# Product tiles of an S5 stage moved from SBUF to PSUM, beside the scan's multipliers

## The chip, the cores and the metric

The kernel runs on one core of a Trainium2 chip. The metric is device time of one execution, in microseconds (us). Engines: PE (TensorE), DVE (VectorE), ACT (ScalarE), POOL (GpSimd); SP is SyncE, whose queue issues all DMAs here. SBUF is the working memory; PSUM is where PE writes, eight banks of 512 float32 columns per partition.

## The reference

Two layers over a latent stream and a context stream of 256 tokens each, 1024 features. Layer 0 mixes tokens by a bidirectional diagonal complex state space (S5): 64 groups of 16 channels with 64 complex states each.

```
a_bar = exp(lam * dt)
b_bar = ((a_bar - 1) / lam)[..., None] * B
h[l]  = a_bar * h[l - 1] + b_bar @ u[l]        # both directions
y     = real(C @ h) + D * u;  out = glu(gelu(y) @ w_glu)
```

The context is scanned first; the latents' scan starts from the context's last state. Then comes a squared-ReLU MLP. Layer 1 is a gated delta rule with an MLP of its own. Every sub-layer has an RMS norm, a modulation by rows computed from c (the `ada` products), and a gated residual.

## The kernel before

The stage of interest is the S5 mixer of layer 0, some 300 us out of the whole. Tokens are cut into 64 chunks of 8 positions, 32 of the context and 32 of the latents, and the work goes by 8 batches of 8 groups.

- `s5_powers` (line 549) computes the powers a^1 .. a^8 (`pw`) and the inputs' factors (`eb`) on DVE. Its last lines allocate the tile `scan`, one PSUM bank, and write a^8 into its first 256 columns by eight small copies (real part and signed imaginary part, per half of the pairs); the tile `scanm`, 256 columns in SBUF, is for the scan's products.
- `s5_we` (line 706) spreads a batch's factors over the partitions by matmuls, into PSUM (`ebx`).
- `s5_w` (line 713) makes, per batch and direction, the tile `W` of 8 positions x 8 groups x 16 channels by `mul_bc` (line 686). That runs twice over half of the positions, 512 columns each time: wtmp = ebx[re] x bc, W = ebx[im] x bc, W = W + wtmp. `wtmp` is one SBUF tile. There are 32 such triples, all on DVE. A small ACT copy takes one position of each W for later (`W0`).
- `s5_in` (line 730) transposes W on PE (`sint`), copies it out by ACT (`Sin`), multiplies it by the tokens U (`xin`), and ACT copies the chunk inputs into X.
- `s5_v` (line 773) makes the outputs' powers V by the same three operations, 1024 columns each, on POOL, with all operands in SBUF (`vtmp`, `bcC`, `ec`). The next batch's `bcC` is loaded into a ring of two tiles.
- `s5_k` (line 790) multiplies V and W0 into strips, stores a strip to DRAM (`kd`), and loads it back eight times, shifted (`Kt`). There is one strip tile; four rounds, for two batches each. Products of Kt and U (`yl`) are the chunks' own part of the outputs.
- `s5_scan` (line 891) goes over the chunks, 63 steps, all on DVE. A step is eight operations of 64 columns: four products m = X[n] x a^8 (`scanm<-X,scan`), then four sums X[n + 1] += m (`X<-X,scanm`), two per half of the pairs.
- `s5_out` (line 909) multiplies the states by V (`yp`), per batch and stream; the context's outputs need the first 31 steps, the latents' all 63. A DVE transpose (`yT`) and a split in two (`y_split`, `yl<-yT,yh`) follow, then the GLU, whose weights are split into a high half on ACT (`whi`) and a low half (`wlo`) on POOL and DVE.

Every operation is recorded by one helper, so all stand under line 254; the rows are read by tile names. The order of the work on each engine is fixed when the program is built: `drive` emits the steps of the tasks in the order in which they could start by a rough clock, each with a priority (the scan 0, outputs 1, `s5_w` 3, `s5_in` 4, `s5_v` 5, strips 7), and a planner then orders each engine's queue by its own model of time. At run time every queue is strictly in order. In `s5_phase` (line 1241) a first part runs to the end of the chunk inputs; a second part has the scan, the rest of V and of the strips, and the context's outputs.

## Time and profile before

| what | us |
|---|---|
| median of 3 runs | 1667.96 |
| lowest, highest | 1667.34, 1669.84 |
| span of the profiled execution, first to last instruction | 1666.9 |

| engine | busy us | share of the span |
|---|---|---|
| PE | 1475.8 | 89% |
| DVE | 1148.8 | 69% |
| ACT | 761.4 | 46% |
| POOL | 663.2 | 40% |

The times are those of whole executions; the span is what one profiled execution took between its first and last instruction, and every duration below comes from that one. Busy shares are means over stages that differ; a stretch of the timeline says more. A wait that the profile shows on an engine holds up all that stands behind it in that engine's queue.

### The profile page before, as it was taken

The numbers are of one execution on the slowest core, as the hardware profiler recorded it, in microseconds if no ns is written. First come the engines' busy times: TensorE is split into PE (matmuls) and PEld (weight loads), VectorE is DVE, ScalarE is ACT, GpSimd is POOL, SyncE is SP. The second block draws the span as 40 slices with busy tenths as digits, with TensorE's granted clock in tenths as the row PEclk, the third lists the DMA queues.
The fourth block names the chain that finished last, engine by engine and source line by source line (L and its number), as shares of the span: only waits on it lengthen the run. The fifth ranks groups of instructions, "written<-read, shape, count | busy, mean of one in ns | idle before, by whom it ended". The sixth has DMA issues, their size and how long they took to land.

```text
span 1666.9 us, 31459 instructions
## 1 busy us (share of the span) xinstructions
PE 1475.8 (89%) x12370; PEld 1122.1 (67%) x12370; DVE 1148.8 (69%) x2267; ACT 761.4 (46%) x1637; POOL 663.2 (40%) x510
## 2 busy tenths in 40 slices
PE   6794386998999999997978898989898999989998
PEld 2464255776777777786766676767676665679997
DVE  7997879774333334337999868587769775667666
ACT  3242162644223222224455755665556764554443
POOL 3988012452333333333675734442425310014342
PEclk8797688898999999998988999999999999999999
DMA  9684743354454545521322211111111111545552
GB/s 287 216 278 90 99 135 114 116 195 140 139 183 163 176 155 172 172 105 65 97 70 73 68 56 55 52 46 39 58 52 52 50 56 48 171 147 184 181 199 89
DMA packets 76789, 201.77 MB, mean 121 GB/s; under 512 B 8544, under 2 KB 28768, under 8 KB 76384
## 3 DMA queue, kind: packets, MB, share of 16 engines
q1 hardware_dynamic: 76640, 199.75, 38.0%
q8 instruction: 97, 1.59, 0.4%
q14 instruction: 52, 0.43, 0.1%
HBM read 192.71 MB, written 7.01 MB: 120 GB/s over the span
## 4 chain that ended last, share of the span: by engine, by line
PE 61%; DVE 20%; issue 5%; ACT 5%; DMA 4%; POOL 3%; SPq 1%; POOLq 0%; DVEq 0%; ACTq 0%
PE w L254 31%; PE proj L254 8%; PE c L254 6%; DVE cacc L254 4%; PE wo L254 3%; PE ada L254 2%; PE glu L254 2%; DVE X L254 2%; DVE vc L254 1%; DVE U L254 1%; SPq L254 1%; DMA kd<-strip 1%; DVE W L254 1%; DVE gt L254 1%; PE op L254 1%
## 5 line engine op out<-in xcount | busy, mean ns | idle before, releaser
L254 ACT CAST whi<-wraw 128x1024 fp32r<-128x1024 f32 x221 | 225.6, 1045 | 262.3 <-PE w L254 139.8
L254 POOL TENSOR_TENSOR wlo<-wraw,whi 128x512 fp32r<-128x512 f32 x129 | 182.5, 1433 | 281.5 <-ACT whi L254 242.7
L254 DVE TENSOR_TENSOR wlo<-wraw,whi 128x1024 fp32r<-128x1024 f32 (+1 forms) x189 | 221.2, 1197 | 77.8 <-ACT whi L254 77.4
L254 PE MATMUL w<-hh,whi 128*128 128x256 f32 (+1 forms) x512 | 170.5, 336 | 0.0
L254 PE MATMUL w<-hl,whi 128*128 128x256 f32 (+1 forms) x512 | 169.0, 332 | 0.0
L254 PE MATMUL w<-hh,wlo 128*128 128x256 f32 (+1 forms) x512 | 168.5, 331 | 0.0
L254 POOL TENSOR_TENSOR sq<-rl 128x512 f32<-128x512 f32 (+1 forms) x64 | 62.2, 973 | 217.8 <-ACT rl L254 214.0
L254 PE MATMUL w<-whi,h1h 128*128 128x512 f32 x384 | 148.9, 395 | 0.0
L254 PE MATMUL w<-whi,h1l 128*128 128x512 f32 x384 | 148.5, 390 | 0.0
L254 PE MATMUL w<-wlo,h1h 128*128 128x512 f32 x384 | 148.4, 389 | 0.0
L254 PE MATMUL proj<-hh,whi 128*128 128x256 f32 (+1 forms) x360 | 133.0, 369 | 11.3 <-ACT pp L254 8.6
L254 DVE TENSOR_TENSOR ma<-w,g 128x512 f32<-128x512 f32 x96 | 65.3, 687 | 102.3 <-PE w L254 102.2
L254 PE MATMUL proj<-hh,wlo 128*128 128x256 f32 (+1 forms) x360 | 128.0, 356 | 1.1 <-POOL wlo L254 1.1
L254 PE MATMUL proj<-hl,whi 128*128 128x256 f32 (+1 forms) x360 | 128.9, 358 | 0.0
L254 DVE SCALAR_TENSOR_TENSOR cacc<-pp,cw,cacc 128x520 f32<-128x520 f32 (+1 forms) x128 | 114.3, 895 | 11.4 <-ACT cacc L254 9.9
L254 POOL TENSOR_TENSOR xr<-xr,ma 128x512 f32<-128x512 f32 x56 | 80.4, 1439 | 96.8 <-DVE ma L254 96.8
L254 PEld LDWEIGHTS w<-hh,whi 128*128 128x128 f32 x512 | 98.0, 192 | 18.5 <-DVE wlo L254 4.2
L254 DVE TENSOR_TENSOR h1l<-sq,h1h 128x512 fp32r<-128x512 f32 (+1 forms) x64 | 35.5, 555 | 107.4 <-POOL sq L254 104.9
L254 ACT ACTIVATE v<-c,vsc 64x128 f32<-64x128 f32 x224 | 80.6, 362 | 54.0 <-PE c L254 46.5
L254 PEld LDWEIGHTS w<-hl,whi 128*128 128x128 f32 x512 | 98.1, 192 | 10.6 <-issue 1.9
L254 PEld LDWEIGHTS w<-hh,wlo 128*128 128x128 f32 x512 | 97.8, 191 | 9.8 <-issue 0.8
L254 POOL TENSOR_TENSOR rstd<-ms,mhalf 128x1 f32<-128x1 f32 (+2 forms) x22 | 17.3, 787 | 190.2 <-DVE ms L254 190.2
(312 smaller groups left out, 3584.6 us busy)
## 6 DMA issues: line engine op xcount, KB each, us to landing
wraw<-in_w_dram SPq DMA_DIRECT2D x128, 512.0 KB, 4.2
adaw<-in_ada_w_dram SPq DMA_DIRECT2D x92, 512.0 KB, 4.4
wraw<-in_w_in_dram SPq DMA_DIRECT2D x48, 512.0 KB, 3.3
wraw<-in_w_glu_dram SPq DMA_DIRECT2D x32, 512.0 KB, 3.5
wraw<-in_w_out_dram SPq DMA_DIRECT2D x16, 512.0 KB, 3.3
Kt<-kd SPq DMA_DIRECT2D x32, 128.0 KB, 6.5
X<-grd SPq DMA_DIRECT2D x32, 128.0 KB, 3.2
V<-in_ada_w_dram SPq DMA_DIRECT2D x4, 512.0 KB, 6.7
```

The costliest lines, as they stand in the source:

```text
L254: r = f(*args, **kw)
```

## The change

The tile `wtmp` of `s5_w` becomes a PSUM tile that shares the ring of one with `scan`. The scan's products `sm` go into columns 256 to 511 of the `scan` bank, whose columns 0 to 255 hold a^8. Since the bank serves `wtmp` first, the eight copies of a^8 move out of `s5_powers` into a task of their own, `s5_a8`, behind the last `s5_w`. The SBUF tiles `wtmp` (512 columns) and `scanm` (256 columns) are gone. Nothing is computed in another way. The diff, cut to these lines (elsewhere it drops comments alone):

```diff
         cmul(eb[:, 1:8], pw[:, 0:7], eb[:, 0], 7)
-        sc = self.ps.tile([128, 512], F32, name="scan", tag="scan", bufs=1)
+    def s5_a8(self):
+
+        V, pw = self.nc.vector, self.pw
+        sc = self.bank("scan", "scan", bufs=1)
         self.a8 = sc[:, 0:256].rearrange("p (k h r d g) -> p k h r d g", k=2, h=2, r=2, d=2)
-        self.sm = self.long.tile([128, 256], F32, name="scanm").rearrange("p (h k e) -> p h k e", h=2, k=2)
+        self.sm = sc[:, 256:512].rearrange("p (h k e) -> p h k e", h=2, k=2)
         for hf in range(2):
...
             V.tensor_copy(self.a8[:, 1, hf, 1], half(1))
+        yield
...
         for d in range(2):
             yield from self.Wslots.take()
-            tmp = E.tile([128, 8, 4, 16], F32, name="wtmp", bufs=1)
+            tmp = self.bank("wtmp", "scan", bufs=1).rearrange("p (g t c) -> p g t c", g=8, t=4)
             W = self.W[b, d] = E.tile([128, 8, 8, 16], F32, name="W", bufs=NW)
...
             ins.append(T(k.s5_in(b), 4, [ws[b], u] + ins[-2:-1], "tensor"))
+        a8 = T(k.s5_a8(), 3, [ws[-1]], "vector")
...
-        rest = drive(k.clock, [lds, a0, a1, xn, u] + we + ws + ins + Ec + list(V.values()) + list(Kk.values()), until=ins + Ec)
+        rest = drive(k.clock, [lds, a0, a1, xn, u, a8] + we + ws + ins + Ec + list(V.values()) + list(Kk.values()), until=ins + Ec + [a8])
```

## Rows read from the trace of the kernel before

**Rows 1.** The page's first line.
```profile
span 1666.9 us, 31459 instructions
```
**Rows 2.** Stretches: us; busy PE, PEld, DVE, ACT, POOL (x instructions); PE clock; DMA share; GB/s.
```profile
75.00:121.00 46.00, 45.80 (x527) 29.92 (x527) 44.62 (x53) 21.35 (x60) 39.83 (x18) 0.91 0.70 237
...
141.00:218.00 77.00, 26.65 (x634) 21.47 (x630) 62.74 (x284) 12.33 (x27) 18.65 (x9) 0.65 0.61 85
218.00:281.00 63.00, 48.04 (x355) 33.75 (x348) 62.23 (x251) 28.25 (x56) 15.43 (x12) 0.84 0.40 134
281.00:375.00 94.00, 87.18 (x599) 68.19 (x598) 73.89 (x112) 51.98 (x88) 48.60 (x40) 0.95 0.47 154
```
**Rows 3.** Chain of waits, 0 to 420 us: start, length, what.
```profile
135.78 3.80 DMA bcC<-in_bc_dram
141.18 9.90 DMA kd<-strip
...
210.93 3.64 PE yl L254 x64
```
**Rows 4.** Timeline of DVE: start, us, operation, count [idle before <- releaser].
```profile
140.45 0.80 DVE L254 TENSOR_TENSOR scanm<-X,scan 128x64 f32<-128x64 f32 x4 [9.05 <-ACT X L254]
141.18 5.67 DVE L254 TENSOR_TENSOR X<-X,scanm 128x64 f32<-128x64 f32 x4
...
160.98 0.76 DVE L254 TENSOR_TENSOR X<-X,scanm 128x64 f32<-128x64 f32 x4
...
218.34 0.45 DVE L254 STREAM_TRANSPOSE yT<-yg 128x256 f32<-128x256 f32 x1 [14.59 <-ACT yg L254]
```
**Rows 5.** Stretches, instructions that touch scanm alone: us, DVE busy (x), clock, DMA.
```profile
210.00:282.00 72.00, 45.56 (x218) 0.81 0.36 119
```
**Rows 6.** Groups of DVE, 26 to 132 us: count | busy us, mean ns | idle before.
```profile
L254 DVE TENSOR_TENSOR W<-W,wtmp 128x512 f32<-128x512 f32 x32 | 44.0, 1375 | 1.0
L254 DVE TENSOR_TENSOR wtmp<-ebx,bcB 128x512 f32<-128x512 f32 x32 | 22.1, 690 | 1.3
```
**Rows 7.** Timeline of DVE, three places in the W stage.
```profile
62.55 8.56 DVE L254 TENSOR_TENSOR U<-U,md 128x1024 f32<-128x1024 f32 x4
71.03 2.82 DVE L254 TENSOR_TENSOR W<-W,wtmp 128x512 f32<-128x512 f32 x1
...
95.15 0.69 DVE L254 TENSOR_TENSOR W<-W,wtmp 128x512 f32<-128x512 f32 x1
```
**Rows 8.** Groups of POOL, 27 to 136 us, then 142 to 160.5 us.
```profile
L254 POOL TENSOR_TENSOR V<-V,vtmp 128x1024 f32<-128x1024 f32 x12 | 32.3, 2689 | 0.7
L254 POOL TENSOR_TENSOR V<-ec,bcC 128x1024 f32<-128x1024 f32 x14 | 31.7, 2285 | 6.0 <-DMA bcC<-in_bc_dram 5.6 <-issue 0.4
...
L254 POOL TENSOR_TENSOR V<-V,vtmp 128x1024 f32<-128x1024 f32 x4 | 9.4, 2340 | 0.2
...
L254 POOL TENSOR_TENSOR V<-ec,bcC 128x1024 f32<-128x1024 f32 x2 | 4.0, 2034 | 0.0
```
**Rows 9.** Timeline of DVE, copies of a^8 into the scan bank.
```profile
21.14 0.65 DVE L254 COPY scan<-pw 128x32 f32<-128x32 f32 x3
...
22.06 0.20 DVE L254 COPY scan<-pw 128x32 f32<-128x32 f32 x1
```
**Rows 10.** Timeline of ACT, 60 to 90 us.
```profile
59.82 0.39 ACT L254 COPY md<-mod 128x256 f32<-128x256 f32 x1 [1.17 <-PE mod L254]
...
73.89 0.30 ACT L254 COPY W<-W 128x128 f32<-128x128 f32 x1 [9.74 <-DVE W L254]
```
**Rows 11.** Timeline of PE, two waits.
```profile
74.78 1.12 PE L254 MATMUL sint<-consts,W 128*128 128x128 f32 x4 [3.69 <-ACT X L254]
...
258.94 0.79 PE L254 MATMUL glu<-wlo,yh 128*128 128x512 f32 x1 [8.23 <-DVE wlo L254]
```
**Rows 12.** The scan's sums on DVE, 161 to 203 us, then 218 to 281.4 us.
```profile
L254 DVE TENSOR_TENSOR X<-X,scanm 128x64 f32<-128x64 f32 x124 | 23.7, 250 | 0.0
...
L254 DVE TENSOR_TENSOR X<-X,scanm 128x64 f32<-128x64 f32 x110 | 28.5, 314 | 0.0
```

## The prediction

> **What bounds the kernel now.** I read the share of busy time by stretch first [rows 1, 2]. After 281 us TensorE (PE) is busy 87.2 of 94 us and stays so; what happens before that is the state space stage, and a microsecond won or lost there is handed on. Three stretches differ. From 75 to 121 us PE is busy 45.8 of 46 us, so it sets the pace. From 141 to 218 PE is busy 26.7 of 77 us: something else does. From 218 to 281 VectorE (DVE) is busy 62.2 of 63 us.

> The chain of waits says what sets the middle stretch [rows 3]. The load of `bcC` for the last batch leaves at 135.78, when GpSimd (POOL) has read what lay in its tile; the store of the first strip leaves at 141.18; then four rounds of storing a strip to DRAM and loading it back as `Kt` run one after another, and the last `yl` product starts at 210.93. DVE has nothing to do with that: its queue stands idle for 14.59 us before the first output transpose at 218.34 [rows 4]. So the steps of the scan that stand ahead of it, all but the last 27 of 63 (218 records after 210 us, eight to a step [rows 5]), end 14.6 us early already.

> What the change is about shows in the time of one form. The 32 sums W = W + wtmp cost 1375 ns each, the products wtmp of the same size 690 [rows 6]. The product reads one operand from PSUM, the sum reads both from SBUF. The one sum that ran while POOL waited for a load (95.15) took 0.69 [rows 7]. POOL pays too: its products take 2.28 us before 136 us and 2.03 after 142, its sums 2.69 and 2.34 [rows 8]. In the scan the four sums of a step took 5.67 us at 141 and 0.76 at 161, when POOL had stopped [rows 4].

> **The change, part by part.**

> *wtmp in PSUM.* The sum then reads one SBUF operand, as the product does that keeps 0.69 us beside a busy POOL. DVE gains 32 x (1.375 - 0.69) = 21.9 us, little of it directly: PE sets the pace there, and DVE waited 9.05 us at 140 for ScalarE (ACT) in any case [rows 4]. Is a sum with a PSUM operand dearer? The product from PSUM takes 690 ns, the free sum from SBUF 0.69 us [rows 6, 7]: I take nothing. [...] Is writing the product there dearer? A 32-column copy into that bank takes 0.20 us [rows 9]; a column costs (690 - 250) / 448 = 1.0 ns [rows 6, 12], which leaves 0.17 for its start, against 0.18 of the product: nothing.

> What reaches the path is POOL's part and one jam. The jam: at 71.03 us a sum takes 2.82 us beside POOL [rows 7]; ACT, which copies a piece of W, stands 9.74 us for it, and the copies that PE needs stand behind that, so PE idles 3.69 us before 74.78 [rows 10, 11]. The multiplications of U, ahead of that sum on DVE, can start 2.4 us earlier than 62.55, since their factor was there at 60.2 [rows 7, 10], and the sum is 2.1 shorter: PE's full stretch moves by some 4.4 us. The loads of bcC stand on SyncE's queue behind weight loads that wait for PE, so POOL's last wait for one, at 111 us, moves by the same 4.4. From there to 135.76 POOL does 11 ops, eight of them slowed by 0.35 to 0.4 us (a sum takes 2.69 in place of 2.34) [rows 8]: 3.0 more. POOL gains 7.4, PE 4.4; the strip's store needs ACT, whose queue stands until bcC lands and then copies what PE made. I take **6.4 us** for the store at 141.18. Bounds: 3.0 (PE stays put) and 7.4. The DRAM rounds behind it keep their length, so the first transpose moves by the same.

> *The factors a^8 later.* Eight small ops move from 17 to 22 us to the place behind the last W sum. They issue no DMA and pass nothing on SyncE or POOL. At 0.23 us each they are 1.8 us in DVE's idle 9.05 us before 140.45 [rows 4, 9]; without that cover they would cost 1.8.

> *The scan's products in the bank of its factors.* Three effects.

> First, its sums read one SBUF operand. In the hidden steps that buys nothing: they had 14.6 us to spare. From 218 to 281 the 110 sums take 314 ns, against 250 without POOL [rows 12]: 110 x 64 ns = **-7.0 us**, all on DVE's full queue.

> Second, a wait is added. The eight copies of a^8 go to different columns of this one bank, and they don't overlap: three take 0.65 us, one 0.20, so each starts about 0.03 after the end of the last [rows 9]. The scan's ops, to and from different columns in SBUF, overlap: an op of 0.25 us starts 0.17 after the one before (four in 0.76) [rows 4]. I read it as an order kept by bank. Then each product waits for the op ahead of it (products write the bank, sums read it), and so does the first sum; sum behind sum does not. That is five places of eight, each 0.28 us in place of 0.17, or 0.55 us a step: 1.36 becomes 1.91. The first 36 steps then take 69 us, from about 134 to 203, still 9 us ahead of the first transpose at 212. The last 27 cost 27 x 0.55 = **+14.9 us**. Behind the waiting op on DVE stand the transposes, the splits of y and the low halves `wlo` of the GLU weights, for which PE waited 8.23 us at 258.94 [rows 11]. The other 33 ops of that stretch, where they fall into one of the five places, hide its wait: 33 x 5/8 x 0.11 = **-2.3**. Fewer steps may fit ahead of the first transpose, since the planner sees slower ones: 31 must, 36 do; I take one less, **+1.9** (bounds 0 and 9.6).

> Third, a product now reads and writes one bank. No row has that. Below: nothing, as copies into it cost nothing more. Above: its 64 columns a second time, 64 ns, which is 108 x 0.064 = 6.9 us late in the scan. I take nothing, by the copies; a gain is excluded, as the columns stay as many.

> *SBUF.* 3 KB per partition become free, so later tiles may lie over others; no row prices that, and with the planner's changed order I allow 3 us either way.

> **Sum.** The scan's end: -6.4 - 7.0 + 14.9 - 2.3 + 1.9 = +1.1 us. After it PE has 6.8 us of idle time in 94 [rows 2]; I let it take a quarter of what the tail adds (7.5), so 5.6 arrive: -6.4 + 5.6 = **-0.8 us**. The profiled execution's span is 1666.9 [rows 1], 1.1 below the median of the runs, 1667.96; the predicted time is 1667.96 - 0.8 = **1667.2 us**. A measurement of this kernel can tell about 0.2%, 3.3 us, from no change, so I forecast none.

> **Rivals.**

> *Faster, by the front.* PE's GLU work may not feel the tail: the planner sets each `wlo` by its own clock, and with waits in the scan there are more openings for it. PE's 8.23 us at 258.94 shrink, a later end of the scan finds PE still at work, and 6.4 less 1 remain: 1662.6. For it: PE stands idle 15 us between 218 and 281 [rows 2]. Against: all that DVE does there is in one queue. If order is kept by column and not by bank, the tail gains too: -6.4 - 7.0 x 0.75 = -11.7, 1656.3; against it stand the copies. Chance 0.36, 0.08 of it for the second.

> *Slower, by the tail.* The latents' steps of the scan set the end. The place is 218 to 281, where DVE is full. It decides from the step time at which the tail eats the front: 6.4 / 0.75 = 8.5 us, so 1.36 + (8.5 + 7.4) / 27 = 1.95 us a step, and I stand at 1.91. With the dearer products (+0.26 a step) and 3.0 at the front it is -3.0 + 7.5 + 6.9 = +11.4: 1679.4. For it: nothing hides DVE there. Against: the copies' price. Chance 0.20.

> *It does not do what it says.* If a W sum waits for POOL because of what it writes to SBUF and not because of a second SBUF input, no gain is left, and 14.5 of waits arrive: 1682.5. The products of W, half of which write W itself beside the busy POOL, speak against it; 0.04. That a sum from PSUM is as dear as one beside POOL now (314 in place of 250 ns), 108 x 0.064 x 0.75 = 5.2 us, against the rows, has 0.04 as well, at 1672.4. [...]

> **How the numbers follow.** No change 0.36, between 1664.6 and 1671.3; faster 0.36; slower 0.20 + 0.04 + 0.04 = 0.28. The forecast lies between the two others because a gain of 6 and a loss of 6 are set against each other. The range reaches into both: 1656 (the whole gain of the front and of the tail) to 1678 (nearly the slower rival's full price).

> **What would show it.** In the new profile the 32 W sums at 0.69 us and POOL's ops at 2.0 and 2.34 before 136 us; the ACT wait of 9.74 gone; the first strip's store near 134.8; the scan's step near 1.9 us with products that no longer overlap; idle time of DVE before the first transpose, near 212; the scan's end near 282. The forecast is wrong if the strip's store stays at 141 (then slower), if a step keeps 1.36 us (faster), or if it takes over 2.1 (slower).

## The result, and the profile after

The changed kernel takes 1690.95 us (median of 4 runs, 1690.22 to 1692.39) against 1667.65 (4 runs, 1667.01 to 1669.84): ratio 1.0141, 95% interval 1.0127 to 1.0156. It is 23.3 us slower, beyond the end of the range. The span of its profiled execution is 22.9 us longer.

First the page's first line of the changed kernel, and its stretches with the columns of [rows 2].

```profile
span 1689.8 us, 31481 instructions
```

```profile
75.00:121.00 46.00, 45.28 (x586) 28.26 (x580) 37.93 (x64) 23.12 (x64) 37.79 (x19) 1.00 0.83 281
...
141.00:218.00 77.00, 22.47 (x438) 17.54 (x438) 40.91 (x177) 7.58 (x18) 8.91 (x5) 0.61 0.70 122
218.00:281.00 63.00, 44.91 (x367) 30.94 (x368) 59.15 (x204) 32.00 (x62) 15.50 (x12) 0.81 0.18 64
281.00:375.00 94.00, 70.67 (x512) 54.10 (x511) 82.46 (x209) 44.70 (x78) 38.45 (x34) 0.91 0.35 118
```

From 141 to 218 DVE is busy 40.9 us where it was 62.7, and from 281 to 375 PE is busy 70.7 where it was 87.2 [rows 2]. So the loss begins on DVE, inside the scan, and PE pays later.

The part before the scan did what the change was for. The groups of DVE from 26 to 132 us, which answer to [rows 6], then POOL's from 27 to 126 us, which answer to [rows 8]:

```profile
L254 DVE TENSOR_TENSOR wtmp<-ebx,bcB 128x512 f32<-128x512 f32 x32 | 22.3, 698 | 2.9 <-DMA bcB<-in_bc_dram 1.7
L254 DVE TENSOR_TENSOR W<-W,wtmp 128x512 f32<-128x512 f32 x32 | 22.0, 686 | 1.0
...
L254 POOL TENSOR_TENSOR V<-V,vtmp 128x1024 f32<-128x1024 f32 x12 | 29.5, 2458 | 0.7
L254 POOL TENSOR_TENSOR V<-ec,bcC 128x1024 f32<-128x1024 f32 x14 | 28.2, 2035 | 7.7 <-DMA bcC<-in_bc_dram 5.0 <-PE ada L254 2.6
```

A W sum takes 686 ns in place of 1375. The DMA queue of the changed kernel shows what that moved: the last load of `bcC` leaves at 125.79, the first strip's store at 130.04 (135.78 and 141.18 before [rows 3]).

```profile
125.79 0.33 SPq L254 DMA_DIRECT2D bcC<-in_bc_dram  x1
130.04 0.68 SPq L254 DMA_DIRECT2D kd<-strip  x1
```

So the scan can start 11 us earlier, and does. Now DVE's timeline in the changed kernel, from the scan's start to the first output transpose:

```profile
129.31 1.21 DVE L254 TENSOR_TENSOR scan<-X,scan 128x64 f32<-128x64 f32 x4 [12.96 <-ACT X L254]
130.55 0.82 DVE L254 TENSOR_TENSOR X<-X,scan 128x64 f32<-128x64 f32 x4
...
170.23 1.19 DVE L254 TENSOR_TENSOR scan<-X,scan 128x64 f32<-128x64 f32 x4
171.45 0.77 DVE L254 TENSOR_TENSOR X<-X,scan 128x64 f32<-128x64 f32 x4
172.26 0.27 DVE L254 TENSOR_TENSOR scan<-X,scan 128x64 f32<-128x64 f32 x1
204.91 0.17 DVE L254 SCALAR_TENSOR_TENSOR modc<-mcol,vecs 128x16 f32<-128x16 f32 x1 [32.38 <-ACT mcol L254]
205.00 0.87 DVE L254 TENSOR_TENSOR scan<-X,scan 128x64 f32<-128x64 f32 x3
...
229.97 0.45 DVE L254 STREAM_TRANSPOSE yT<-yg 128x256 f32<-128x256 f32 x1 [0.72 <-ACT yg L254]
```

Two things are new. The four products of a step take 1.19 us in place of 0.74 to 0.80, and a step 2.03 in place of 1.36. And in the middle of step 22 stands a stranger: `modc`, an operation of 0.17 us that makes the scale of the MLP's norm (`mod_cols`, line 1025). Its input `mcol` comes from the last columns of the modulation, which PE multiplies behind the last `yl` products. Nothing of the scan runs ahead of it, so the scan stands 32.4 us behind an operation whose result is first read at 356.3. In the kernel before, `modc` stands behind 41 steps, at 227.00, and waits for nothing. (Steps are counted here by their products: `modc` now stands behind 21 steps and the first of the four products of the next, which is written 21.25.) The first transpose starts at 229.97 instead of 218.34 [rows 4], and the scan ends at 324.8 instead of 281.0 (its end is given everywhere as the start of its last sum).

### The profile page after: what moved, and what is told of

It is laid out like the page before. It is cut to its first block, busy times and chain, and to the rows that moved or that the text cites. A ratio compares the mean times of both kernels' runs of the same rounds, so it can differ in the third digit from the quotient of the medians.

```text
span 1689.8 us, 31481 instructions
## 1 busy us (share of the span) xinstructions
PE 1479.8 (88%) x12370; PEld 1124.4 (67%) x12370; DVE 1135.7 (67%) x2267; ACT 765.1 (45%) x1637; POOL 655.0 (39%) x510
## 4 chain that ended last, share of the span: by engine, by line
PE 63%; DVE 21%; ACT 5%; DMA 5%; issue 4%; SPq 1%; POOL 1%; POOLq 0%; DVEq 0%; ACTq 0%
PE w L254 31%; PE proj L254 8%; PE c L254 7%; DVE cacc L254 3%; PE ada L254 3%; PE wo L254 3%; DVE scan L254 2%; DVE X L254 2%; PE glu L254 2%; DVE wlo L254 1%; DVE U L254 1%; SPq L254 1%; PE qs L254 1%; DMA adaw<-in_ada_w_dram 1%; DVE gt L254 1%
## 5 line engine op out<-in xcount | busy, mean ns | idle before, releaser
L254 POOL TENSOR_TENSOR wlo<-wraw,whi 128x512 fp32r<-128x512 f32 x129 | 182.0, 1430 | 281.0 <-ACT whi L254 231.9
```

The source lines that it names most:

```text
L254: r = f(*args, **kw)
```

## The experiments

Theory: the place of `modc` is the loss, and beside it front and tail of the prediction nearly cancel. Rival: 63 steps, each 0.67 us longer, are 42 us, about what the scan ends later; the stall stands where DVE would have waited anyway.

The first four kernels hold `modc` in program order behind the scan and then make the two halves of the change one by one.

**The change with modc held back.** Edit:

```diff
-        self.nc.vector.scalar_tensor_tensor(o, self.mcol[l][:, vec], 1.0,
+        i = self.nc.vector.scalar_tensor_tensor(o, self.mcol[l][:, vec], 1.0,
...
+        if (l, vec) == (0, 4):
+            self.pin(i)
```

> The changed kernel, but the small op modc = mod_cols(0, 4) is held in program order on VectorE, so that it stands behind the scan and not after 21.25 of its steps. All arithmetic is kept. Theory (the stall): in the changed kernel VectorE stands 32.4 us ahead of modc, from 172.5 to 204.9, while 42 steps of the scan are queued behind it. Without it the 33 steps ahead of the first output transpose end at 129.3 + 33 x 2.03 = 196, the last yl product stays near 198 to 201, and the first transpose starts near 206 in place of 229.97. The tail keeps its 95 us, the scan ends near 301 in place of 324.8, the span falls by 20 to 24 us, to 1666 to 1670. Rival (the step): 63 steps at 2.03 in place of 1.36 us are 42 us, which is all of the 43.6 us by which the scan ends later; the stall only stands where VectorE would have waited for TensorE, the scan ends within 6 us of 324.8 and the time stays within 5 us of 1691.

Measured: 1668.77 us against 1665.21, ratio 1.0022 (1.0001 to 1.0044). The stall is gone; DVE waits at the transpose, as in the kernel before. Its timeline:

```profile
196.40 0.77 DVE L254 TENSOR_TENSOR X<-X,scan 128x64 f32<-128x64 f32 x4
197.20 0.27 DVE L254 TENSOR_TENSOR scan<-X,scan 128x64 f32<-128x64 f32 x1
211.90 0.45 DVE L254 STREAM_TRANSPOSE yT<-yg 128x256 f32<-128x256 f32 x1 [14.43 <-ACT yg L254]
```

The scan ends at 306.7, 18 us earlier than in the changed kernel, which is what the first transpose moved (229.97 to 211.90). The rival is out. The transpose came 6 us later than I had put it, because of ACT's queue, whose order had changed as well:

```profile
206.69 0.26 ACT L254 COPY mcol<-adat 128x16 f32<-128x16 f32 x2 [0.74 <-PE adat L254]
206.82 3.35 ACT L254 COPY Hs<-X 64x256 f32<-64x256 f32 x8
```

The copies `Hs`, which the outputs need, now stand behind the late `mcol` copy; in the kernel before they started at 199.87, ahead of it. So the stall's twin on ACT is still in this kernel.

**Only wtmp in PSUM, modc held back.** Edit, beside the one above:

```diff
-        self.sm = sc[:, 256:512].rearrange("p (h k e) -> p h k e", h=2, k=2)
+        self.sm = self.long.tile([128, 256], F32, name="scanm").rearrange("p (h k e) -> p h k e", h=2, k=2)
```

> Only the first half of the change: wtmp in PSUM and the factors a^8 copied later; the scan's products stay in SBUF, modc held behind the scan. All arithmetic is kept. Theory (the front is a gain of its own): the last yl product moves from 210.93 to about 198 as in the changed kernel, the scan's step stays at 1.36 us once GpSimd is done, the first transpose starts near 206 in place of 218.34 and the scan ends 10 to 12 us before 281.25; the time is 8 to 12 us below the kernel before, 1656 to 1660. Rival (the front is swallowed): the GLU's weights or TensorE take back what the front gives, the time stays within 3 us of 1667.7.

Measured: 1654.31 us, ratio 0.9935 (0.9910 to 0.9960), 10.9 us below. First transpose at 207.36, the scan's end at 270.7, as expected.

**Only the scan's products in PSUM, modc held back.** Edit, beside the hold:

```diff
-            tmp = self.bank("wtmp", "scan", bufs=1).rearrange("p (g t c) -> p g t c", g=8, t=4)
+            tmp = E.tile([128, 8, 4, 16], F32, name="wtmp", bufs=1)
```

> Only the second half of the change: the scan's products in the bank of its factors; wtmp stays in SBUF, modc held behind the scan. All arithmetic is kept. Theory (tail price as the prediction built it, with the step at 2.03): first transpose near 218 as before; 30 steps behind it at 2.03 us against 27 at 1.36 are 61 - 37 = 24 us, less 7 us of sums that GpSimd no longer slows and 2 us hidden by other ops: the scan ends 13 to 20 us after 281, the time is 10 to 16 us above the kernel before, 1678 to 1684. Rival (other work hides the steps): under 5 us above it.

Measured: 1676.83 us, ratio 1.0064 (1.0040 to 1.0088), 11.6 us above. The first transpose is at 218.39, so the price is all in the tail. But the scan ends at 313.1, 32 us behind the kernel before and not 13 to 20. DVE's timeline splits these 32 us. Counted from start to start, the scan's own operations behind the first transpose take 57.5 us where they took 43.9, which is 13.6 more, near the 15 of the sum above. The other 18.5 are work for the GLU that DVE now does before the scan's end and did after it.

**The kernel before with modc held back**, the control.

> The kernel before with modc held behind the scan and nothing else: the control for the three others. There modc started at 227.0 without a wait, after 41 steps. Both theories: within 1.5 us of the kernel before; if more, the three others are to be read against this one.

Measured: 1663.09 us, ratio 0.9993 (0.9971 to 1.0015): no difference that this interval would show. The four together, as ratios to the kernel before:

| modc held back | products of the scan in SBUF | in PSUM |
|---|---|---|
| wtmp in SBUF | 0.9993 | 1.0064 |
| wtmp in PSUM | 0.9935 | 1.0022 |

Front -0.6 to -0.7%, tail +0.7 to +0.9%, both +0.2 to +0.3%. The change itself stood at +1.4%; what the hold takes away is 1.2%, or 20 us.

**Only wtmp in PSUM, modc where the planner puts it.**

> Only the first half of the change (wtmp in PSUM, a^8 later, the scan's products in SBUF), with modc where the scheduler leaves it, after 41 steps of the scan as in the kernel before. All arithmetic is kept. Theory (the stall comes with the scan's products alone): modc finds mcol ready or nearly so, nothing stands 30 us, and the run is as the one with modc held back, ratio 0.9935 within 0.003, so 8 to 13 us below the kernel before. Rival (an earlier scan meets mcol too early, whatever its step costs): a wait of over 8 us ahead of modc, and half of the gain or more is gone.

Measured: 1655.73 us, ratio 0.9951 (0.9934 to 0.9967), some 8 us below. `modc` stands behind 41 steps at 215.83, without a wait. An earlier scan alone doesn't move it in the queue.

**Only the scan's products in PSUM, modc where the planner puts it.**

> Only the second half of the change (the scan's products in PSUM, wtmp in SBUF), with modc where the scheduler leaves it, after 21.25 steps. All arithmetic is kept. Theory (the stall again): the scan reaches modc near 181, mcol is there near 213, so VectorE stands some 32 us; 12 steps follow, and the first transpose is near 238.5, 20 us behind the 218.39 of the run with modc held back; ratio to the kernel before 1.0064 + 0.012 = 1.018, 29 us above it. Rival (most of the wait is absorbed later): ratio below 1.010.

Measured: 1697.68 us, ratio 1.0210 (1.0181 to 1.0239). The stall is there again, after 21.25 steps; DVE's timeline:

```profile
215.68 0.18 DVE L254 SCALAR_TENSOR_TENSOR modc<-mcol,vecs 128x16 f32<-128x16 f32 x1 [34.80 <-ACT mcol L254]
```

Against the same kernel with `modc` held back it costs 1.5%, 24 us.

**a^8 in SBUF.** The changed kernel, `modc` held back, and

```diff
-        self.a8 = sc[:, 0:256].rearrange("p (k h r d g) -> p k h r d g", k=2, h=2, r=2, d=2)
+        self.a8 = self.long.tile([128, 256], F32, name="a8s").rearrange("p (k h r d g) -> p k h r d g", k=2, h=2, r=2, d=2)
```

> The changed kernel with modc held back, and the factors a^8 copied to SBUF, so that a product of the scan writes PSUM but reads none of it; its sums read PSUM as before. All arithmetic is kept. Theory (order by bank): products still follow each other without overlap, four in 1.1 to 1.25 us, the step stays between 1.9 and 2.05 us once GpSimd is done, the time within 4 us of the run with a^8 in PSUM. Rival (a product that reads and writes one bank pays for it): four products in 1.0 us or less, a step of 1.8 us or less, and the time 4 to 8 us lower.

Its timeline of DVE, at the scan's start and 40 us later:

```profile
130.94 8.15 DVE L254 TENSOR_TENSOR scan<-X,a8s 128x64 f32<-128x64 f32 x4 [14.25 <-ACT X L254]
139.12 0.78 DVE L254 TENSOR_TENSOR X<-X,scan 128x64 f32<-128x64 f32 x4
...
170.74 1.20 DVE L254 TENSOR_TENSOR scan<-X,a8s 128x64 f32<-128x64 f32 x4
171.97 0.79 DVE L254 TENSOR_TENSOR X<-X,scan 128x64 f32<-128x64 f32 x4
172.79 1.20 DVE L254 TENSOR_TENSOR scan<-X,a8s 128x64 f32<-128x64 f32 x4
```

Measured: four products in 1.20 us, a step in 2.05, where they took 1.19 and 2.03 with a^8 in PSUM: reading and writing one bank cost nothing here, as the prediction took it. The time missed: 1680.69 us, ratio 1.0091 (1.0057 to 1.0125), some 11 us (0.7%) above the run with a^8 in PSUM and not within 4. Now the products read two SBUF operands beside POOL, the first four take 8.15 us, and the scan ends at 316.4, 9.7 us later than with a^8 in PSUM.

**Products in two banks.** As in the last kernel, with the two halves' products in banks of their own:

```diff
-        self.sm = sc[:, 256:512].rearrange("p (h k e) -> p h k e", h=2, k=2)
+        s2 = self.bank("scan2", "scan2", bufs=1)
+        self.sm2 = [x[:, 0:128].rearrange("p (k e) -> p k e", k=2) for x in (sc, s2)]
...
-        k.ps = cs.enter_context(k.tc.tile_pool(name="ps5", bufs=4, space=bass.MemoryType.PSUM))
+        k.ps = cs.enter_context(k.tc.tile_pool(name="ps5", bufs=3, space=bass.MemoryType.PSUM))
```

> As the run with a^8 in SBUF, but the products of the two halves lie in two banks, so that each op's forerunner is in the other bank (one of the four shared banks of the stage is given up for it, which changes TensorE's work before 141 us). All arithmetic is kept. Theory (order by bank): products overlap again, four in 0.7 to 0.85 us, the step is 1.4 to 1.5 us after 165 us. Rival (a product that goes to PSUM is dearer in itself): the products stay at 0.27 us or more from start to start and the step at 1.9 us. The time itself is not to be compared.

```profile
169.88 0.77 DVE L254 TENSOR_TENSOR scan<-X,a8s 128x64 f32<-128x64 f32 x4
170.56 0.77 DVE L254 TENSOR_TENSOR X<-X,scan 128x64 f32<-128x64 f32 x4
171.24 0.78 DVE L254 TENSOR_TENSOR scan<-X,a8s 128x64 f32<-128x64 f32 x4
```

From DVE's timeline: four products in 0.77 us, a step in 1.36. With the products in SBUF they took 0.74 to 0.79 and a step 1.36. So neither a product into PSUM nor a sum out of it was dearer here; the order by bank is the whole of the 0.67 us. The programs built from these kernels say who keeps it: waits on VectorE's own counter that the instructions carry. In the changed kernel all four products and the first sum of a step wait for the operation directly ahead of them. In the kernel before no operation of a step does that: two of the products and the four sums wait for one further back. With two banks all eight operations wait, but for the one before the last, and they overlap.

The time, 1685.34 us, was not meant for comparison. Its excess over the changed kernel with `modc` held back does not come from the scan, which ends at 287.8 and not at 306.7: PE's last product for the norm ahead of layer 1 starts at 778.6, 5.6 us earlier than there (784.2), and its first for the norm of layer 1's MLP at 1492.3, 22.6 us later (1469.7). So it is lost in layer 1, and why stays open.

**The stall alone.** The kernel before, with the second product of step 22 ordered behind `modc`:

```diff
-                    V.tensor_tensor(m(k, hf), at(n, hf, k == 1), self.a8[:, k, hf], op=OP.mult)
+                    i = V.tensor_tensor(m(k, hf), at(n, hf, k == 1), self.a8[:, k, hf], op=OP.mult)
+                    if (n, k, hf) == (21, 0, 1):
+                        self.step21 = i
...
+            self.tc.add_manual_dep(self.step21.ins, i.ins.name, mybir.DependencyInfo(
+                mybir.DependencyClass.NoSync, mybir.DependencyReason.DATA), reason="modc first")
```

> The kernel before with nothing of the change, but with the place that modc has in the changed kernel: the second product of the scan's step 22 is ordered behind modc on VectorE, so that modc stands after 21.25 steps and not after 41. All arithmetic is kept. Theory (the place alone costs): the scan reaches it near 183, mcol comes near 218.5 (7.75 us after the last group of yl products starts at 210.9, as in the run with the second half of the change and modc held back), so VectorE stands some 35 us; 9.75 steps at 1.36 us, the copies Hs and one product later the first transpose starts near 237.5, 19 us behind 218.34. The time is 14 to 20 us above the kernel before, ratio 1.0085 to 1.012. Rival (the stall hurts only together with the dearer steps): the cheap steps make up for it, ratio below 1.004.

```profile
184.99 0.27 DVE L254 TENSOR_TENSOR X<-X,scanm 128x64 f32<-128x64 f32 x1
217.20 0.18 DVE L254 SCALAR_TENSOR_TENSOR modc<-mcol,vecs 128x16 f32<-128x16 f32 x1 [31.94 <-ACT mcol L254]
...
235.70 0.45 DVE L254 STREAM_TRANSPOSE yT<-yg 128x256 f32<-128x256 f32 x1
```

Measured: 1684.78 us, ratio 1.0122 (1.0092 to 1.0153), 21.2 us above the kernel before, a little over the end of what was expected. With cheap steps, and nothing of the change in it, the stall costs the same.

**The changed kernel on the same chip.**

> The changed kernel itself, on the same chip as the kernel before with the stall alone. Theory: ratio 1.0141 as in the first comparison, so the place of modc (1.0085 to 1.012) is three quarters of the loss, and what is left beside it is the sum of front and tail, 0 to 0.5%. Rival: the two stalls differ by more than 0.4%, so that the stall's price hangs on the step's.

Measured: 1691.66 us against 1663.59, ratio 1.0164 (1.0139 to 1.0189). The stall alone is 1.2 of these 1.6%: three quarters, as expected. The stall's price lay between 1.2 and 1.5% in all four comparisons: with dear steps 1.2 (the first comparison) and 1.4 (this one), both against the run with `modc` held back, and 1.5 with wtmp in SBUF; with cheap steps 1.2. What is left beside it, 0.4%, agrees with the 0.2% of the run with `modc` held back, given the intervals.

## Why the prediction was wrong

Its forecast was no change, from a front gain and a tail loss that cancel. With `modc` held back they do cancel, at +0.2%. It left out one thing that costs 20 to 24 us.

**The step that failed** is the planner's order. The prediction saw that "the planner sees slower ones", asked only how many steps would still fit ahead of the first transpose, took "one less", and allowed the changed order "3 us either way". The question to ask was which other operations the planner would let in among the slower steps. `modc` stands after 41 steps with the products in SBUF, after 21.25 with them in one bank, whether wtmp is in PSUM or not. In the program of the two-bank kernel without the hold, which was built and not run, it stands after 36. So it goes with the order by bank. That the planner takes each wait between dependent operations for free time of DVE, and expects `mcol` much too early, is my reading of this and not shown; no run separates the two. That `modc` would have to wait if it came earlier was to be read in the trace of the kernel before. ACT's timeline there, then DVE's:

```profile
226.78 0.26 ACT L254 COPY mcol<-adat 128x16 f32<-128x16 f32 x2
```

```profile
227.00 0.18 DVE L254 SCALAR_TENSOR_TENSOR modc<-mcol,vecs 128x16 f32<-128x16 f32 x1
```

The copies of its input start 0.2 us ahead of it: it had no room to move up. In the run with the stall alone these copies came 10 us earlier (216.98), and `modc` still stood 31.9 us for them. I had not looked at what else stood among the steps.

The other steps:

*wtmp in PSUM.* Right: 686 ns a sum, as against 0.69 us. POOL's products came to 2035 ns as predicted, its sums to 2458, between [rows 8] and the 2.34 I took. A sum from PSUM was no dearer by itself: four take 0.77 us, four from SBUF 0.76 [rows 4].

*The front.* Mis-sized: -6.4 for the first strip's store, -11.1 measured; -10.9 in the time of the run with wtmp alone (some -8 where `modc` is not held). PE's part was put at 4.4; the `bcC` load that left at 105.67 leaves at 96.30, 9.4 earlier. The missing 5 us are a wait that ended earlier than I had put it (the matmuls behind it start at 68.59 in place of 74.78, 6.2 us and not 4.4) and, for the rest, mostly the clock. The stretches 75 to 80 and 80 to 85 us, of the kernel before and then of the changed one (columns as in [rows 2]):

```profile
75.00:80.00 5.00, 5.00 (x50) 4.43 (x51) 4.83 (x8) 2.19 (x7) 5.00 (x3) 0.50 0.22 67
80.00:85.00 5.00, 5.00 (x52) 3.39 (x48) 4.86 (x7) 2.01 (x5) 5.00 (x3) 0.65 0.01 3
```

```profile
75.00:80.00 5.00, 5.00 (x58) 2.81 (x54) 4.77 (x8) 1.34 (x5) 4.92 (x4) 1.00 0.70 215
80.00:85.00 5.00, 5.00 (x28) 2.40 (x26) 4.83 (x8) 1.58 (x6) 4.84 (x3) 1.00 0.99 363
```

PE is busy throughout in both, but behind its wait of 3.69 us [rows 11] the granted clock was 0.50 and 0.65 of full clock; after the change it is 1.00. At full clock those 10 us would have done 5 x 0.50 + 5 x 0.35 = 4.2 us more, an estimate. On PE's timeline the lead of 6.2 us has grown to 9.2 at the next long group of `ada` products (74.23 in place of 83.44), about the lead of that load. I had counted the wait and not the slow clock behind it.

*a^8 later.* Right: the copies end at 116.35, DVE then waits 12.96 us.

*The tail.* The mechanism was right, order by bank in five places of eight; the size was not. A product behind another starts 0.31 us after it, not 0.28, so a step costs 0.67 more and not 0.55. The sums gained as predicted: behind 207 us they take 265 ns, against 335 with their products in SBUF. But 33.25 steps stand ahead of the first transpose, not 35.

Between the runs with `modc` held back and wtmp in PSUM, the scan's end moves from 270.7 to 306.7, by 36.0 us. The first transpose is 4.5 of it (`Hs` behind `mcol` on ACT). The scan's own operations behind it, from start to start, take 57.5 us in place of 45.8, which is 11.7. The rest, 19.7, is other work that DVE now does before the scan's end. The groups of DVE, first in the kernel before (218 to 281.4 us), then with both halves and `modc` held back (207 to 308 us), show it; with wtmp alone the counts up to the scan's end are those of the kernel before:

```profile
L254 DVE TENSOR_TENSOR wlo<-wraw,whi 128x512 fp32r<-128x512 f32 x10 | 8.9, 897 | 0.0
L254 DVE TENSOR_TENSOR xr<-xr,gm 128x256 f32<-128x256 f32 x2 | 0.8, 410 | 0.0
```

```profile
L254 DVE TENSOR_TENSOR wlo<-wraw,whi 128x512 fp32r<-128x512 f32 x19 | 19.6, 1034 | 0.0
L254 DVE TENSOR_TENSOR xr<-xr,gm 128x256 f32<-128x256 f32 x8 | 7.0, 879 | 0.0
```

Most of that work is early and not extra: by 308 us DVE has made 18 `wlo` with wtmp alone (868 ns each) and 19 with both halves (1034 ns). So the price of the tail is 4.5 + 11.7 = 16.2 us. The prediction's terms for the tail summed to 7.5. Of the missing 8.7 us, 4.5 is the first transpose, which it did not move; 3.1 are steps that no longer fit ahead of it (5.0 in place of 1.9); and 1.1 is the dearer step (6.7 in place of 5.6).

Of these 16.2 us some 11 (by the spans) to 14 (by the medians) reach the end, two thirds to nine tenths, around the three quarters I had taken. The stretches 206 to 270, 270 to 308 and 308 to 375 us of the kernel with both halves and `modc` held back, then of the one with wtmp alone, show where PE loses them:

```profile
206.00:270.00 64.00, 52.06 (x398) 36.14 (x398) 55.56 (x181) 35.77 (x68) 17.56 (x14) 0.89 0.41 140
270.00:308.00 38.00, 17.85 (x74) 12.83 (x78) 36.43 (x116) 8.61 (x13) 14.96 (x14) 0.80 0.38 124
308.00:375.00 67.00, 64.14 (x506) 51.48 (x503) 53.04 (x86) 40.77 (x72) 29.91 (x24) 0.96 0.42 133
```

```profile
206.00:270.00 64.00, 47.39 (x394) 33.61 (x387) 62.32 (x248) 29.07 (x57) 18.50 (x12) 0.87 0.40 131
270.00:308.00 38.00, 32.70 (x342) 22.71 (x341) 31.77 (x62) 23.90 (x46) 17.16 (x13) 0.96 0.38 122
308.00:375.00 67.00, 61.00 (x316) 51.05 (x318) 48.73 (x64) 34.76 (x54) 33.01 (x31) 0.97 0.55 180
```

PE loses 14.9 us of work between 270 and 308, while it waits for the latents' states. It had done 4.7 more before, and does 3.1 more after, so that 7.0 are missing at 375. Another 3.5 are missing by 450 (69.9 us of work in place of 73.4), and the spans differ by 10.7. While the scan lasts PE has the context's GLU to do, so it does not lose all that the scan does. A tail price half as large as the measured one gave 5.6 where 11 to 14 were due, and the front's error was of like size the other way: that the two cancel is half luck.

*The rivals.* "Slower by the tail" named the right sign and not the cause: its deciding step of 1.95 us was passed at 2.03, and yet the time with `modc` held back is 1.0022. "Faster by the front" is what the first half does by itself, and that kernel (wtmp in PSUM, the scan's products left in SBUF) beats both: 0.9951 as the planner orders it, 0.9935 with `modc` held back, intervals that overlap.

## What to carry to other kernels

Where a planner fills gaps, a slower operation also changes what stands between its fellows: before costing such an edit, list the small operations emitted later for the same engine, and ask of each when its input comes; one that is early in the queue and late in its data holds up all behind it, and holding it in program order costs nothing (0.9993 here). Small operations of one engine that follow each other in one PSUM bank lost their overlap here even on different columns, by waits that the program carries (0.31 us from start to start in place of 0.17); give neighbours in the queue different banks, or leave them in SBUF. And a delay is worth what waits for it: 17.4 us at the first transpose, in the run with the stall alone, cost 21.2 us, while 36 us at the scan's end cost 11 to 14, since 19.7 of them were other work, most of it only done earlier.

## What the runs showed of the hardware that was not expected

Beside POOL, a product with two SBUF operands took about as long as one operation of POOL. With a^8 in SBUF the scan's first four products of 64 columns took 8.15 us, 2.04 each; from 121 to 141 us POOL was busy 19.53 of 20 us in that run, and up to 50 us its products had taken 2.03 each and its sums 2.37. From 141 to 206 POOL was busy 9.13 of 65 us, and the scan's fourth four, at 152.29, took 1.18. With a^8 in PSUM, in the changed kernel, the first four took 1.21, at 129.31. Whether each product waited for one operation of POOL is not shown.
